# Row parts of the PE array taken in turn on two PSUM banks

## The chip, the core and the metric

The program runs on one core of a Trainium2 chip. The core has five engines that run side by side and wait for each other by semaphores: TensorE (PE, matmuls), VectorE (DVE), ScalarE (ACT), GpSimd (POOL) and SyncE (SP, which starts DMA transfers). Matmuls write to PSUM, which the kernel uses as eight banks of 128 x 512 float32; DVE and ACT read the results from there. The metric is the device time of one execution in microseconds (us), the median of three runs.

## What is computed

Two stacked networks over a sequence of 512 tokens of width 1024, all in float32. The first block has two layers: a dilated band attention beside an attention over 256 memory rows, then a gated delta rule beside the same memory attention, each followed by a gated feed-forward. The second block mixes a gated linear attention, a state space scan and a sparse attention. Four places matter here:

```
# delta stage, for each of 6 heads, 8 chunks of 64 tokens and 2 directions
a = lmat + eye(64)                       # lmat strictly lower triangular
sol = triangular_solve(a, rhs, lower=True, unit_diagonal=True)

# dilated band attention, 12 heads of 64 in 3 groups
logits = einsum('nbqhd,nbkhd->nbhqk', qs, kw)

# memory attention, 4 heads of 64 over 256 rows, in both layers
logits = einsum('bshd,bmhd->bhsm', q, k)

# gated linear attention, 4 heads of 32
scores = einsum('bhnid,bhnjd,bhnijd->bhnij', qh, kh, decay)
```

## The kernel before

Weights stream from memory through three raw buffers (SP issues the transfers), are split into a high and a low part (ACT L239, DVE L258) and multiplied by the activations in three matmuls for each product (L267 to L269, PSUM tiles named `bk`). These projections, feed-forwards and output products are most of PE's work. Between them stand the small stages.

**What sets the order.** Nothing is scheduled by the tools: a planner in the kernel (`Flow`) runs generators. Each `yield "PE", cost` (or DVE, ACT, POOL) asks for an engine with an estimated cost in us, `yield "get", "lv"` asks for a PSUM bank of a set, `F.put` gives it back. The planner takes the request that can start first and, among those within 0.1 us, the one with the smallest `late`. The order it finds is the program's order on each engine. The eight banks are divided into sets: mm 2 (projections), px 3, lv 3. All small stages here take their banks from lv.

**The array's parts.** A matmul with 64 contracted rows uses half the rows of PE's array (partitions 0 to 63 or 64 to 127: a row part); one with 64 output columns uses half its columns. Heads of 64 lie on one row part each, heads of 32 on a quarter of the rows.

**The inverse (`inverse`, L1480).** The unit triangular systems of a head are inverted by doubling: U holds the inverses' diagonal blocks, and each of five levels computes products of Ln and U (L1528, 16 matmuls of 64x64x64: eight on row part f=0 into one bank, then eight on f=1 into another), transposes U (L1509, four 128x128, a third bank `tt`), copies both (ACT: `xs` twice 256 columns L1536, `T` 512 columns L1516), multiplies the transposes by the products (L1547, again eight matmuls on one row part into one bank, then eight on the other into another) and writes the result into U under a mask (DVE, L1552, once for each bank). A last half level (L1565, L1571, L1585) makes the off-diagonal half for `Uf`. There is one U at a time (`inv=1`), so the six heads follow each other. The chains over chunks (`chain`), the convolutions (`hn`, L1316), the memory attention and the projections of later heads run in between.

**The other three.** The attention's unit (L653) and the memory attention (L851) take for each of two row parts h a bank, two matmuls (columns 128, 192 or 256), and DVE's pass over it. The linear attention's scores (L2121) take for each of four heads on 32 rows a bank and eight matmuls of 32x64x64 (four at level 6).

Of the kernel before, what the change touches and what calls it, by code (L numbers as in the profile page):

```python
# [26 lines left out]
F32 = mybir.dt.float32  # L27
# [28 lines left out]
class Flow:  # L56
# [42 lines left out]
    def run(self):  # L99
        while self.threads:  # L100
            again = True
            while again:
                again = False
                for t in list(self.threads):
                    kind, *arg = t["req"]
                    value = None
                    if kind == "get" and any(self.sets[n] for n in arg):
                        value = min((n for n in arg if self.sets[n]), key=lambda n: min(self.sets[n])[0])
                        tok = min(self.sets[value])
                        self.sets[value].remove(tok)  # L110
                    elif kind == "wait" and all(e["tok"] for e in arg):
# [47 lines left out]
class K:  # L159
# [375 lines left out]
    def attention(self, F, W, eX, eM, eB, at, e2):  # L535
# [98 lines left out]
        def unit(g, t):  # L634
# [202 lines left out]
    def mem_attention(self, F, i, q, tile_p, tile_t, aux, acc):  # L837
        nc = self.nc
        for t in range(4):
# [5 lines left out]
            for h in range(2):  # L845
                rr = slice(h * 64, h * 64 + 64)
                yield "get", aux
                yield "PE", 0.86
                s = self.psum(aux, "ms_s").rearrange("p (c k) -> p c k", c=2)
                for c in range(2):  # L850
                    nc.tensor.matmul(s[:, c, :], q[rr, c, ts], self.memK[i][rr, c, :], start=True, stop=True)  # L851
                yield "DVE", 0.6
# [309 lines left out]
    def deltanet(self, F, wev, order, eX, res):  # L1162
# [313 lines left out]
        QQ = 0.063  # L1476

        def inverse(h, r):
# [23 lines left out]
            def transposes():  # L1502
                yield "get", "lv"
                tt = yield "PE", 4 * TR, tU
                t = self.psum("lv", "tt")
# [5 lines left out]
                return t, tt  # L1511

            def copyT(t, tt):
                tT = yield *act(512), tt
                T = late["pool"].tile([P, 2, 2, 2, 64], F32, name="T")
                nc.scalar.activation(T.rearrange("p d n f q -> p (d n f q)"), t, AF.Copy)  # L1516
                F.put("lv", tT)
                return T, tT
            dn8 = lambda x: x[:, :256].rearrange("p (d n q) -> p d n q", d=2, n=2)
            for l in range(1, 6):  # L1520
                X2, tx, xs = [], [], []
                for f in range(2):
                    yield "get", "lv"
                    tx.append((yield "PE", 8 * QQ, tU))
                    x = self.psum("lv", "x2")
                    for d in range(2):
                        for c in range(4):
                            nc.tensor.matmul(dn8(x)[HB[c % 2], d, c // 2, :], Ln[d][HB[f], c, HB[f]],  # L1528
                                             U[HB[f], d, c, :], start=True, stop=True)
                    X2.append(x)  # L1530
                t, tt = yield from transposes()
                ts = []
                for f in range(2):
                    ts.append((yield *act(256), tx[f]))
                    xs.append(late["pool"].tile([P, 2, 2, 64], F32, name=f"xs{f}"))
                    nc.scalar.activation(xs[f], dn8(X2[f]), AF.Copy)  # L1536
                    F.put("lv", ts[f])
                T, tT = yield from copyT(t, tt)
                ty, ys = [], []
                for par in range(2):  # L1540
                    yield "get", "lv"
                    ty.append((yield "PE", 8 * QQ, *ts, tT))
                    y = self.psum("lv", "y2")
                    for d in range(2):
                        for n in range(2):
                            for f in range(2):
                                nc.tensor.matmul(dn8(y)[HB[f], d, n, :], T[HB[par], d, n, f, :],  # L1547
                                                 xs[f][HB[par], d, n, :], start=True, stop=True)
                    ys.append(y)
                for par in range(2):  # L1550
                    tU = yield "DVE", 0.34, ty[par]
# [5 lines left out]
            xs = late["pool"].tile([P, 2, 2, 64], F32, name="xs0")  # L1557
            X2, tx, ts = [], [], []
            for d in range(2):
                f = 1 - d  # L1560
                yield "get", "lv"
                tx.append((yield "PE", 4 * QQ, tU))
                x = self.psum("lv", "x2")
                for c in range(4):
                    nc.tensor.matmul(dn8(x)[HB[c % 2], 0, c // 2, :], Ln[d][HB[f], c, HB[1 - f]], U[HB[f], d, c, :],  # L1565
                                     start=True, stop=True)
# [1744 lines left out]
```

## Time and profile before

| | us |
|---|---|
| median of 3 runs | 1822.44 (1821.06 to 1831.11) |
| profiled execution | 1820.18 |
| its span, first to last instruction | 1818.5 |
| attention stage, about | 78 to 262 |
| delta stage, first products to the last `Uf` | 720 to 1018 |
| linear attention's scores | 1494 to 1560 |

A row of PE's instructions in order has the start, the time from its start to the end of the last of it, the line, the operation, what is written from what, the used rows*columns of the array, the moving operand and the count; neighbouring instructions of a line are one row. An fp32 matmul is two instructions there. A row of a stretch has busy us and, in brackets, the instructions that touch it. PEld is PE's loading of the stationary operand, which overlaps with PE.

### The profile page before, as it was taken

The numbers are of one execution on the slowest core, as the hardware profiler recorded it, in microseconds if no ns is written. First come the engines' busy times: TensorE is split into PE (matmuls) and PEld (weight loads), VectorE is DVE, ScalarE is ACT, GpSimd is POOL, SyncE is SP. The second block draws the span as 40 slices with busy tenths as digits, with TensorE's granted clock in tenths as the row PEclk, the third lists the DMA queues.
The fourth block names the chain that finished last, engine by engine and source line by source line (L and its number), as shares of the span: only waits on it lengthen the run. The fifth ranks groups of instructions, "written<-read, shape, count | busy, mean of one in ns | idle before, by whom it ended". The sixth has DMA issues, their size and how long they took to land.

```text
span 1818.5 us, 30258 instructions
## 1 busy us (share of the span) xinstructions
PE 1762.9 (97%) x12031; PEld 1465.8 (81%) x12031; DVE 976.7 (54%) x1997; ACT 768.2 (42%) x1844; POOL 337.9 (19%) x496
## 2 busy tenths in 40 slices
PE   6999989999999998999999999999999999999999
PEld 5988779888888887887878778888888888887787
DVE  6333556323333378665776466454433566467673
ACT  6434435332222355555655344333223352344671
POOL 5200001000000021121122252275540032210000
PEclk9999999999999999999999999999999999999999
DMA  6422133333333233101011155344333253552112
GB/s 202 137 58 82 47 115 93 117 93 101 97 93 95 92 116 82 36 25 47 25 36 36 36 145 152 100 145 136 108 106 93 86 154 91 156 139 70 33 36 82
DMA packets 211982, 167.85 MB, mean 92 GB/s; under 512 B 21996, under 2 KB 183036, under 8 KB 211840
## 3 DMA queue, kind: packets, MB, share of 16 engines
q1 hardware_dynamic: 203808, 154.39, 28.9%
q0 software_dynamic: 4560, 9.42, 2.0%
q10 hardware_dynamic: 3472, 2.10, 0.4%
q8 instruction: 95, 1.56, 0.4%
q14 instruction: 47, 0.39, 0.1%
HBM read 152.23 MB, written 13.65 MB: 91 GB/s over the span
## 4 chain that ended last, share of the span: by engine, by line
PE 87%; DVE 7%; ACT 2%; issue 2%; DMA 1%; POOL 1%; ACTq 0%; SPq 0%; DVEq 0%; POOLq 0%
PE bk L267 23%; PE bk L268 22%; PE bk L269 21%; PE x L1528 2%; PE y L1547 2%; PE no L2765 1%; DVE wl L258 1%; DVE hn L1316 1%; PE npT L2748 1%; PE gs L2121 1%; PE tt L1509 1%; PE ms_s L851 1%; DVE hs L934 1%; PE ns L2734 1%; PE ns L2732 1%
## 5 line engine op out<-in xcount | busy, mean ns | idle before, releaser
L258 DVE TENSOR_TENSOR wl<-raw,wh 128x512 fp32r<-128x512 f32 x450 | 315.6, 741 | 372.4 <-ACT wh L239 371.8
L239 ACT ACTIVATE wh<-raw 128x512 fp32r<-128x512 f32 x474 | 272.8, 622 | 549.8 <-PE bk L269 311.1
L267 PE MATMUL bk<-Xh,wl 128*128 128x512 f32 (+2 forms) x1312 | 495.3, 378 | 0.2 <-ACT Xh L943 0.2
L268 PE MATMUL bk<-Xl,wh 128*128 128x512 f32 (+2 forms) x1312 | 478.3, 365 | 0.5 <-DVE Xl L948 0.5
L269 PE MATMUL bk<-Xh,wh 128*128 128x512 f32 (+2 forms) x1312 | 478.5, 365 | 0.0
L267 PEld LDWEIGHTS bk<-Xh,wl 128*128 128x128 f32 (+1 forms) x1312 | 247.2, 188 | 41.6 <-issue 5.1
L269 PEld LDWEIGHTS bk<-Xh,wh 128*128 128x128 f32 (+1 forms) x1312 | 247.0, 188 | 40.1
L268 PEld LDWEIGHTS bk<-Xl,wh 128*128 128x128 f32 (+1 forms) x1312 | 247.5, 189 | 34.8 <-DVE Xl L948 0.9
L267 PE MATMUL bk<-wh,Xl 128*128 128x512 f32 (+1 forms) x424 | 155.5, 367 | 8.5 <-ACT wh L239 3.5
L268 PE MATMUL bk<-wl,Xh 128*128 128x512 f32 (+1 forms) x424 | 146.3, 345 | 0.1
L269 PE MATMUL bk<-wh,Xh 128*128 128x512 f32 (+1 forms) x424 | 146.2, 345 | 0.0
L267 PE MATMUL bk<-wh,Al 128*128 128x512 f32 x352 | 139.7, 397 | 0.0
L268 PE MATMUL bk<-wl,Ah 128*128 128x512 f32 x352 | 139.5, 396 | 0.0
L269 PE MATMUL bk<-wh,Ah 128*128 128x512 f32 x352 | 138.6, 394 | 0.0
L913 POOL TENSOR_TENSOR nc<-ncm,nhalf 128x1 f32<-128x1 f32 x16 | 11.6, 722 | 676.5 <-DVE ncm L911 672.2
L267 PEld LDWEIGHTS bk<-wh,Xl 128*128 128x128 f32 x424 | 85.6, 202 | 21.5 <-issue 4.1
L1085 DVE TENSOR_TENSOR sg<-sg,bk 128x512 f32<-128x512 f32 x44 | 30.2, 687 | 124.2 <-PE bk L269 119.7
L268 PEld LDWEIGHTS bk<-wl,Xh 128*128 128x128 f32 x424 | 85.8, 202 | 7.7 <-DVE wl L258 0.9
L269 PEld LDWEIGHTS bk<-wh,Xh 128*128 128x128 f32 x424 | 85.4, 201 | 8.0
L267 PEld LDWEIGHTS bk<-wh,Al 128*128 128x128 f32 x352 | 66.1, 188 | 16.1
L269 PEld LDWEIGHTS bk<-wh,Ah 128*128 128x128 f32 x352 | 66.0, 188 | 16.0
L268 PEld LDWEIGHTS bk<-wl,Ah 128*128 128x128 f32 x352 | 66.1, 188 | 15.4
(588 smaller groups left out, 2673.2 us busy)
## 6 DMA issues: line engine op xcount, KB each, us to landing
raw<-in_ffn_w_gate_up_dram SPq DMA_DIRECT2D x88, 512.0 KB, 4.0
raw<-in_ffn_w_down_dram SPq DMA_DIRECT2D x44, 512.0 KB, 3.4
raw<-in_dn_w_in_dram SPq DMA_DIRECT2D x27, 512.0 KB, 3.8
raw<-in_att_w_in_dram SPq DMA_DIRECT2D x20, 512.0 KB, 3.8
raw<-in_w_in_dram SPq DMA_DIRECT2D x20, 512.0 KB, 4.2
raw<-in_mem_w_kv_dram SPq DMA_DIRECT2D x8, 512.0 KB, 3.6
raw<-in_att_w_out_dram SPq DMA_DIRECT2D x8, 512.0 KB, 3.5
xd<-x SPq DMA_DIRECT2D x8, 512.0 KB, 3.0
```

The lines of the kernel that those rows point to most:

```text
L239: nc.scalar.activation(wh[:, sl], ev["raw"][:, sl], AF.Copy)
L258: eng.tensor_tensor(wl[:, sl], raw[:, sl], wh[:, sl].bitcast(F32), op=OP.subtract)
L267: mm(out, A[1], B[0], start=first, stop=False, **kw)
L268: mm(out, A[0], B[1], start=False, stop=False, **kw)
L269: mm(out, A[0], B[0], start=False, stop=last, **kw)
L851: nc.tensor.matmul(s[:, c, :], q[rr, c, ts], self.memK[i][rr, c, :], start=True, stop=True)
L934: nc.vector.scalar_tensor_tensor(hh[:, hv[i]], x[:, t, hv[i]], r2, r["gain"][:, hv[i]], op0=OP.mult, op1=OP.mult)
L1085: nc.vector.tensor_tensor(sg, sg, pu, op=OP.mult)
L1316: nc.vector.scalar_tensor_tensor(acc[:, d0:d1], raw[:, d0 + o:d1 + o], cw[:, ti, tap:tap + 1], acc[:, d0:d1], op0=OP.mult, op1=OP.add)
L1509: nc.tensor.transpose(t[:, i:i + P], U[:, d, 2 * n:2 * n + 2, :].rearrange("p c q -> p (c q)"), self.ident)
L1528: nc.tensor.matmul(dn8(x)[HB[c % 2], d, c // 2, :], Ln[d][HB[f], c, HB[f]], U[HB[f], d, c, :], start=True, stop=True)
L1547: nc.tensor.matmul(dn8(y)[HB[f], d, n, :], T[HB[par], d, n, f, :], xs[f][HB[par], d, n, :], start=True, stop=True)
```

## The change

The planner gets a new request, `"two"`, which is granted when a set has two free banks and takes both. At the four places the matmuls of both row parts become one piece of work: they are written in turn, first row part into one bank, second row part into the other.

- Inverse: the 16 first products alternate between the row parts and banks. The transposes of U go into the upper 256 columns of the same two banks (L1523 in the changed file) in place of a third one. ACT then copies each bank whole, products and transposes, into `xT0` and `xT1` (L1530; 384 columns in the last level). The second products (L1544) alternate too.
- Attention, memory attention: both h in one piece, c outside, h inside.
- Linear attention: heads two by two, the pair innermost.
- The planner's costs of these pieces are set lower. In `chain` the addition into `ot` names the other direction's copy as something it waits for.

```diff
+                    elif kind == "two" and len(self.sets[arg[0]]) > 1:
+                        for _ in range(2):
+                            tok = min(self.sets[arg[0]])
+                            self.sets[arg[0]].remove(tok)
...
-            for h in range(2):
-                yield "get", "lv"
-                yield "PE", 2 * 0.0017 * (hi - lo)
-                s = self.psum("lv", "as").rearrange("p (c k) -> p c k", c=2)
-                rr = slice(h * 64, h * 64 + 64)
-                for c in range(2):
-                    nc.tensor.matmul(s[:, c, lo:hi], qT[rr, c, ts], kT[rr, c, k0 + lo:k0 + hi], start=True, stop=True)
-                tk = yield dve(2 * (hi - lo))
+            yield "two", "lv"
+            tp = yield "PE", 2 * 0.0018 * (hi - lo)
+            sh = [self.psum("lv", "as").rearrange("p (c k) -> p c k", c=2) for _ in range(2)]
+            for c in range(2):
+                for h in range(2):
+                    rr = slice(h * 64, h * 64 + 64)
+                    nc.tensor.matmul(sh[h][:, c, lo:hi], qT[rr, c, ts], kT[rr, c, k0 + lo:k0 + hi], start=True, stop=True)
+            for h, s in enumerate(sh):
+                tk = yield *dve(2 * (hi - lo)), tp
...
-        QQ = 0.063
+        QQ = 0.035
...
+            def step(products):
+                yield "two", "lv"
+                tt = yield "PE", len(products) * QQ + 4 * TR, tU
+                b = [self.psum("lv", "x2") for _ in range(2)]
+                for i, at, lhsT, rhs in products:
+                    nc.tensor.matmul(dn8(b[i])[at], lhsT, rhs, start=True, stop=True)
                 for d in range(2):
                     for n in range(2):
-                        i = (2 * d + n) * P
-                        nc.tensor.transpose(t[:, i:i + P], U[:, d, 2 * n:2 * n + 2, :].rearrange("p c q -> p (c q)"),
+                        o = 256 + n * P
+                        nc.tensor.transpose(b[d][:, o:o + P], U[:, d, 2 * n:2 * n + 2, :].rearrange("p c q -> p (c q)"),
                                             self.ident)
...
+                lo = 512 - 256 - 16 * len(products)
+                for i in range(2):
+                    ts.append((yield *act(512 - lo), tt))
+                    z.append(late["pool"].tile([P, S], F32, name=f"xT{i}"))
+                    nc.scalar.activation(z[i][:, lo:], b[i][:, lo:], AF.Copy)
+                    F.put("lv", ts[i])
...
+                xs, T, ts = yield from step([(f, (HB[c % 2], d, c // 2), Ln[d][HB[f], c, HB[f]], U[HB[f], d, c, :])
+                                             for d in range(2) for c in range(4) for f in range(2)])
+                yield "two", "lv"
+                ty = yield "PE", 16 * QQ, *ts
+                ys = [self.psum("lv", "y2") for _ in range(2)]
+                for d in range(2):
+                    for n in range(2):
+                        for f in range(2):
+                            for par in range(2):
+                                nc.tensor.matmul(dn8(ys[par])[HB[f], d, n, :], T[d][HB[par], n, f, :],
+                                                 xs[f][HB[par], d, n, :], start=True, stop=True)
...
-                    yield "get", "lv"
-                    tp = yield "PE", 0.25
-                    p = self.psum("lv", "gs").rearrange("p (u k) -> p u k", k=64)[:, :4]
+                    if not h % 2:
+                        yield "two", "lv"
+                        tp = yield "PE", 0.3 if l == 6 else 0.5
+                        pp = [self.psum("lv", "gs").rearrange("p (u k) -> p u k", k=64)[:, :4] for _ in range(2)]
```

How the order moves, at three places. PE at the first head's first level, before (`x` the first products, the number is the bank's; `tt` the transposes; `y` the second products):

```order
L1528 MATMUL x_5849<-U,Ln_5692 64x64 x4
L1528 MATMUL x_5849<-U,Ln_5814 64x64 x4
L1528 MATMUL x_5861<-U,Ln_5692 64x64 x4
L1528 MATMUL x_5861<-U,Ln_5814 64x64 x4
L1509 MATMUL tt<-ident,U 128x128 x4
L1327 MATMUL pkT<-ident,ktok 128x128 x4
L275 MATMUL rowbc<-ident,gc 128x128 x4
L1547 MATMUL y_5898<-xs_5876,T 64x64
L1547 MATMUL y_5898<-xs_5878,T 64x64
```

and now, from the end of the same products on:

```order
L1519 MATMUL x_5849<-U,Ln_5814 64x64
L1519 MATMUL x_5850<-U,Ln_5814 64x64
L1523 MATMUL x_5849<-ident,U 128x128 x2
L1523 MATMUL x_5850<-ident,U 128x128 x2
L1335 MATMUL pkT<-ident,ktok 128x128 x4
L279 MATMUL rowbc<-ident,gc 128x128 x4
L271 MATMUL bk<-Xh,wl 128x512
L272 MATMUL bk<-Xl,wh 128x512
L273 MATMUL bk<-Xh,wh 128x512
L1544 MATMUL y_5898<-xT_5880 64x64
L1544 MATMUL y_5899<-xT_5880 64x64
```

The products go to two banks (5849 and 5850) by turns instead of eight and eight, the transposes to the same two; a projection stands ahead of the second products where none stood. ACT at the same place, before:

```order
L1311 ACTIVATE hn<-craw,convw 128x512
L1536 ACTIVATE xs_5876<-x_5849 128x256
L1536 ACTIVATE xs_5878<-x_5861 128x256
L1516 ACTIVATE T<-tt 128x512
L1367 ACTIVATE kTh<-pkT 128x512
L1307 ACTIVATE craw<-bk 128x512
```

and now:

```order
L1319 ACTIVATE hn<-craw,convw 128x512
L1530 ACTIVATE xT_5880<-x_5849 128x512
L1530 ACTIVATE xT_5889<-x_5850 128x512
L1375 ACTIVATE kTh<-pkT 128x512
L1315 ACTIVATE craw<-bk 128x512
```

Two copies of 512 columns stand for two of 256 and one of 512. PE at the last head's fifth level, just ahead of its second products, before (`poT` is another head's output; three more projection matmuls stand between the transposes and these rows):

```order
L267 MATMUL bk<-Xh,wl 128x512
L268 MATMUL bk<-Xl,wh 128x512
L269 MATMUL bk<-Xh,wh 128x512
L1327 MATMUL poT<-ident,otok 128x128 x4
L1547 MATMUL y_9641<-xs_9623,T 64x64
```

and now:

```order
L1519 MATMUL x_9527<-U,Ln_9087 64x64
L1519 MATMUL x_9528<-U,Ln_9087 64x64
L1523 MATMUL x_9527<-ident,U 128x128 x2
L1523 MATMUL x_9528<-ident,U 128x128 x2
L1544 MATMUL y_9561<-xT_9553 64x64
```

Ahead of the second products six projection matmuls and a transpose stood; now nothing stands there.

## Rows read from the trace of the kernel before

**Rows 1.** The page: busy time of each engine; the chain that ended last.

```profile
PE 1762.9 (97%) x12031; PEld 1465.8 (81%) x12031; DVE 976.7 (54%) x1997; ACT 768.2 (42%) x1844; POOL 337.9 (19%) x496
PE 87%; DVE 7%; ACT 2%; issue 2%; DMA 1%; POOL 1%; ACTq 0%; SPq 0%; DVEq 0%; POOLq 0%
```

**Rows 2.** Stretches: start:end and length, then busy us (instructions) PE, PEld, DVE, ACT, POOL; clock; DMA.

```profile
720.00:1018.00 298.00, 289.55 (x3436) 236.06 (x3435) 204.81 (x475) 162.97 (x462) 64.81 (x54) 1.00 0.12 35
1494.00:1560.00 66.00, 66.00 (x778) 54.19 (x777) 41.94 (x97) 20.92 (x43) 20.18 (x22) 1.00 0.36 102
```

**Rows 3.** PE's instructions in order: start us, busy us; the last level's products.

```profile
749.60 0.47 PE L1565 MATMUL x<-U,Ln 64*64 64x64 f32 x16
751.98 0.45 PE L1585 MATMUL y<-xs,T 64*64 64x64 f32 x8
```

**Rows 4.** PE's instructions in order, the attention's scores.

```profile
92.14 1.13 PE L653 MATMUL as<-kT,qT 64*128 64x256 f32 x4
94.53 1.13 PE L653 MATMUL as<-kT,qT 64*128 64x256 f32 x8
97.94 0.91 PE L653 MATMUL as<-kT,qT 64*128 64x192 f32 x4
...
144.81 1.16 PE L653 MATMUL as<-kT,qT 64*128 64x128 f32 x8
...
153.83 0.71 PE L653 MATMUL as<-kT,qT 64*128 64x128 f32 x4
```

**Rows 5.** PE's instructions in order, the inverse's first products: a whole pair, a half.

```profile
733.77 0.98 PE L1528 MATMUL x<-U,Ln 64*64 64x64 f32 x32
...
770.08 0.68 PE L1528 MATMUL x<-U,Ln 64*64 64x64 f32 x16
```

**Rows 6.** PE's busy us (instructions) in the delta stage: L1528, then L1547, then L1585.

```profile
720.00:1018.00 298.00, 33.28 (x960) 1.00 0.12 35
720.00:1018.00 298.00, 32.37 (x960) 1.00 0.12 35
720.00:1018.00 298.00, 4.96 (x96) 1.00 0.12 35
```

**Rows 7.** PE, PEld busy us (instructions): two rows of L653, then three of L851.

```profile
78.00:262.00 184.00, 16.03 (x96) 11.72 (x96) 0.98 0.21 64
208.00:262.00 54.00, 4.81 (x32) 3.66 (x32) 0.94 0.13 41
...
78.00:262.00 184.00, 8.92 (x32) 5.35 (x32) 0.98 0.21 64
208.00:262.00 54.00, 3.28 (x12) 2.01 (x12) 0.94 0.13 41
720.00:1018.00 298.00, 9.02 (x32) 5.35 (x32) 1.00 0.12 35
```

**Rows 8.** PE: a memory score, a linear attention's score; all of L2121, as rows 7.

```profile
831.50 1.13 PE L851 MATMUL ms_s<-memK,oT 64*128 64x256 f32 x4
...
1494.60 0.68 PE L2121 MATMUL gs<-gq,gk 32*64 32x64 f32 x16
...
1494.00:1560.00 66.00, 21.75 (x480) 17.32 (x480) 1.00 0.36 102
```

**Rows 9.** Groups on xs, T and U: duration ns min/median/max, first and last start, forms.

```profile
L1536 ACT ACTIVATE xs<-x x60: 357/383/421, 722.3 to 1009.6; 128x256 f32<-128x256 f32 x60
...
L1516 ACT ACTIVATE T<-tt x36: 585/597/618, 723.1 to 1014.8; 128x512 f32<-128x512 f32 x36
...
L1552 DVE COPY_PREDICATED U<-lm,y x60: 430/443/455, 727.2 to 1013.0; 128x256 f32<-128x256 uint8 x60
```

**Rows 10.** A stretch at the attention stage's end, columns as in rows 2.

```profile
208.00:235.00 27.00, 21.66 (x191) 16.84 (x190) 20.90 (x55) 15.39 (x59) 0.00 (x0) 0.94 0.07 21
```

**Rows 11.** A piece of the chain (start, us); a wait (us, times, longest); delta stage.

```profile
794.55 1.68 DVE hn L1316
...
PEld x L1528 <- DVE U L1552: 4.1, 7, 1.9
```

More of the change, by code (lines that the diff above doesn't have):

```diff
@@ L844, in mem_attention @@
             den = self.small.tile([P, 4], F32, name="mden")
[L845 to L852, printed above, removed]
+            yield "two", aux
+            tp = yield "PE", 0.95
+            sh = [self.psum(aux, "ms_s").rearrange("p (c k) -> p c k", c=2) for _ in range(2)]
+            for c in range(2):
+                for h in range(2):
+                    rr = slice(h * 64, h * 64 + 64)
+                    nc.tensor.matmul(sh[h][:, c, :], q[rr, c, ts], self.memK[i][rr, c, :], start=True, stop=True)
+            for h, s in enumerate(sh):
+                yield "DVE", 0.6, tp
                 nc.vector.tensor_reduce(nm[:, h::2], s, axis=AX.X, op=OP.max, negate=True)
@@ L1506, in transposes @@
                 for d in range(2):
                     for n in range(2):
-                        i = (2 * d + n) * P
-                        nc.tensor.transpose(t[:, i:i + P], U[:, d, 2 * n:2 * n + 2, :].rearrange("p c q -> p (c q)"),
+                        o = 256 + n * P
+                        nc.tensor.transpose(b[d][:, o:o + P], U[:, d, 2 * n:2 * n + 2, :].rearrange("p c q -> p (c q)"),
                                             self.ident)
[L1511 to L1518, printed above, removed]
+                z, ts = [], []
@@ L1520, in inverse @@
             for l in range(1, 6):
[L1521 to L1539, printed above, removed]
-                for par in range(2):
[L1541 to L1549, printed above, removed]
@@ L1552, in inverse @@
+                for par in range(2):
+                    tU = yield "DVE", 0.34, ty
                     nc.vector.copy_predicated(U[:, :, par::2, :],
@@ L1556, in inverse @@
             b4 = beta.rearrange("p (d c h) -> p d c h", d=2, c=4)[:, :, :, h]
[L1557 to L1566, printed above, removed]
-                X2.append(x)
-            t, tt = yield from transposes()
-            for d in range(2):
-                ts.append((yield *act(128), tx[d]))
-                nc.scalar.activation(xs[:, d], dn8(X2[d])[:, 0], AF.Copy)
-                F.put("lv", ts[d])
-            T, tT = yield from copyT(t, tt)
+            xs, T, ts = yield from step([(d, (HB[c % 2], 1, c // 2), Ln[d][HB[1 - d], c, HB[d]], U[HB[1 - d], d, c, :])
+                                         for c in range(4) for d in range(2)])
             yield "get", "uf"
@@ L1595, in inverse @@
             r["eU"]["tok"] = max(t, tP)
-            r["n"], r["done"] = 0, set()
+            r["n"], r["done"] = 0, {}
             r["o"] = late["pool"].tile([P, 4, P], F32, name="otok", bufs=2)
@@ L1644, in chain @@
                 if c in r["done"]:
-                    to = yield "DVE", 0.2, to
+                    tc_ = yield "wait", r["done"][c]
+                    to = yield "DVE", 0.2, to, tc_
                     nc.vector.tensor_tensor(ot[:, c, :], ot[:, c, :], o, op=OP.add)
                 else:
-                    r["done"].add(c)
+                    done = r["done"][c] = F.event()
                     to = yield *act(P), to
                     nc.scalar.activation(ot[:, c, :], o, AF.Copy)
+                    done["tok"] = to
                 F.put("lv", to)
```

40 lines of the change are left out of this document (19 added, 21 removed).

## The prediction, made before the run

> **What bounds the kernel now.** I read the page first: TensorE (PE) is busy 97% of the span, and 87% of the chain that ended last goes through it [rows 1]. VectorE (DVE) is busy 54%, ScalarE (ACT) 42%, so the question in each touched stage is whether PE is held up there by its own work. The stretches say yes: over the 298 us of the delta stage PE is busy 289.6, over the 66 us of the linear attention's scores 66.0 [rows 2]. The one exception is the end of the attention stage, where PE is busy only 21.7 of 27 us and DVE 20.9 [rows 10]. The granted clock is 1.00 in the first two stretches, so no clock is to be won or lost there.
>
> Next: what does a small matmul cost PE? In the inverse a matmul uses 64 of the 128 rows and 64 of the 128 columns of the array, and an fp32 matmul is two instructions in the trace. The half step at L1585 (8 instructions, one row part, one bank) occupies PE for 0.45 us. L1565 is 16 instructions, 8 on one row part and 8 on the other, into two banks, and occupies PE for 0.47 us [rows 3]. Twice the work for 0.02 more: **the row parts run side by side when both are within reach.** The attention's scores show the same without any change of code: where two groups of four on *different* row parts happen to stand next to each other (94.53 us; the heads' loop tells the parts) the eight take 1.13 us, as long as the four at 92.14 alone; where two groups on the *same* row part stand together (144.81 us) eight take 1.16 against 0.71 for four of that width, which is one after the other [rows 4]. And a whole pair of the inverse (32 instructions) takes 0.98, while a pair cut by other work takes 0.68 twice [rows 5]: with all of one bank's matmuls first, PE gets to the second row part only when most of the first is done. With perfect overlap a pair should take 0.68 + 0.03 = 0.71 us, where 0.03 is the 0.02 above, rounded up.
>
> **What the new order takes away.** I price every pair at the busy time of one half plus 0.03 us.
>
> - First products (L1528): 33.28 us now for 960 instructions [rows 6]; 30 pairs (6 heads, 5 levels) at 0.71 are 21.3. Gain 12.0.
> - Second products (L1547): 32.37 now, as many pairs, 21.3 afterwards. Gain 11.1.
> - Last level: L1585 4.96 now; six pairs of 0.48 are 2.9. Gain 2.1. L1565 (six times 0.47) is side by side already: no gain.
> - Memory scores: 8.92 + 9.02 us [rows 7]; a half is 1.13 [rows 8], eight pairs of 1.16 are 9.3. Gain 8.6, about half of it in each stage.
> - Attention scores: 16.03 us [rows 7]. Two of its twelve pairs are 192 wide (0.91), two 256 wide (1.13), eight 128 wide (0.71) [rows 4]: 2 x 0.94 + 2 x 1.16 + 8 x 0.74 = 10.1. Gain 5.9.
> - Linear attention's scores: 21.75 us for 32 groups of 0.68 [rows 8]; 16 pairs of 0.71 are 11.4. Gain 10.4. No row here shows two parts of 32 rows side by side, so its ends are 10.4 (as the parts of 64 rows) and 0; I take the first, since its halves run at exactly the pace of the 64-row ones (16 instructions in 0.68 in both).
>
> The sum is 50.1 us of PE's time: 25 from the inverse, 4.4 more in the delta stage from the memory, 10.2 in the attention stage, 10.4 at the scores.
>
> **What it adds and moves.** The transposes of U now go into the second half of the two product banks: the same four instructions behind the products, no cost. The copies: before, two of 0.383 us and one of 0.597 on ACT; now two of 128x512, 0.597 each as the copy to T [rows 9]. That is 0.17 us less ACT work per step, but both now begin behind the transposes, and the second products wait for both. From the last transpose to the second products that makes about 0.2 + 0.6 + 0.6 = 1.4 us (0.2 is the planner's own figure for a hop between engines); from those to the next first products two updates of U at 0.443 [rows 9] and two hops, about 1.3. Whether PE waits depends on what the planner put between. In the changed program's order I counted the other PE work in these gaps, a bk matmul 128x512 at 0.23 and a 128x128 one at 0.11: nearly all hold 1.1 to 3.5 us, as much as is needed, and the total of other work from the first to the last step is as before. Only the last head runs short: one gap of 0 and two near 0.7, because the projections that fill PE are used up ahead of its last two steps. That costs about 3 us. PE waits for the inverse little today (4.1 us for U's update, [rows 11]); I allow 1 us more.
>
> Not everything in the delta stage follows PE. Between heads the chain leaves it for the convolution on DVE (single pieces of 1.7 us, [rows 11]); with less PE work these stretches come to the front oftener: 3 us. In the tail of the attention stage, where DVE and PE take turns, as scores worth 1.9 us and memory scores worth 1.5 fall [rows 10]: 4.81 and 3.28 us there [rows 7], less four pairs of 0.74 and one and a half of 1.16; I count half, so 1.7 are lost. Against 50.1 stand 3 + 1 + 3 + 1.7, and 1.3 for waits inside the first pairs, which the 33.28 contains and which stay: 10 us. **Net 40 us: 1820.2 - 40 = 1780.** The median of the runs shown is 2.3 us above the profiled execution, which is less than the uncertainty of this sum; I leave the number as it is.
>
> The wait in "done" (second direction's addition behind the first one's copy) only tells the planner of an order that the data had already. Nothing is added on the chip.
>
> One thing has to hold for all of this: a matmul on the second row part must be able to start ahead of one that stands before it in the program. In L1565 the program has all eight instructions of the first bank ahead of the second bank's, and 0.47 us for both [rows 3] is possible only so. The Trainium skill says otherwise: by "TensorE: Matmul & The Clock Gate", Part 3, What overlaps and what doesn't, matmuls start and end strictly in program order. By it the result would be the second rival's. The rows disagree with it, and the measurement decides.
>
> **The rivals.**
> 1. *The inverse's own chain becomes the bound of the delta stage.* It is serial (one U, three lv banks); a step has about 0.7 + 0.5 + 1.4 + 0.7 + 1.3 = 4.6 us in it, and the 36 steps make 166 of the 298 us, the rest being PE's other work and the change of heads. For it: DVE pieces on the chain [rows 11], the exhausted fill at the last head. Against: PE busy 97% there and the filled gaps. If two thirds of the delta stage's 29 us stay behind, the time is 1820 - (50 - 19 - 2) = 1791, with bad luck 1800.
> 2. *Alternating parts don't run side by side*, each start waiting for its predecessor's. Then the two instructions of a matmul, 0.058 us apart ((0.68 - 0.45) / 4, from the halves of 16 and 8 instructions on two column parts, [rows 3, 5]), hold up the next part, and a pair takes 0.68 + 8 x 0.058 = 1.14 us. An uncut pair now takes 0.98, a cut one 1.36; in the order of before 43 of the 60 are uncut, which makes 43 x 0.16 - 17 x 0.22 = +3 us, and the scores give back about as much: 1820, no change. The measured pieces speak against it [rows 3, 4].
> 3. *Slower: two banks at once of three lv banks.* A pair starts only when two are free, and the memory attention and the chains' outputs hold single ones (a memory score bank through 1.13 of PE, a maximum and two exponentials). 72 pairs of the inverse stand behind this; it decides from 50 / 72 = 0.7 us of unfilled wait at each, and at 1 us each the time is 1820 - 50 + 72 = 1842. For it: at the third head, where the memory runs, gaps grow to 5 and 6 us in the new order. Against: these are full of other PE work, not empty. The Trainium skill's "TensorEngine Tiling (Array Packing)", Gotcha 1, names this pressure on PSUM; no row here shows its price.
> 4. *All of it arrives*, the off-PE stretches shrinking with PE's, and the order falling well elsewhere: 1820 - 50 = 1770, at best 1765.
>
> **How the numbers follow.** Forecast (1773 to 1787) 0.53; rival 1 (1788 to 1805) 0.24; rival 4 (1764 to 1772) 0.13; rival 2 (1812 to 1824) 0.06; rival 3 0.04. The likeliest's time is 1780. The range takes in rivals 1 and 4 and thereby the zero end of the 32-row parts alone (1790): 1765 to 1803. A measurement of this kernel tells about 0.5% from no change, 9 us: below 1813 lie the first three cases, 0.90; same 0.06; slower 0.04.
>
> **What would show it.** Products of a pair: 32 instructions in about 0.71 us with none of 0.98 or twice 0.68, scores of the linear attention 32 in 0.71, memory scores eight in 1.16. If the pairs are short but the delta stage (298 us) does not shrink to about 276, PE's idle time there or longer waits of the products for ACT or DVE name rival 1. Pairs of 1.1 us name rival 2. Idle PE ahead of the first of a pair, ended by the release of a bank, names rival 3. The forecast is wrong if the stages before and after the touched ones move by more than 5 us, since I gave the reshuffled order there nothing.

## The result and the profile after

The changed kernel takes **1762.9 us** (median of 4 runs, 1761.48 to 1763.83) against 1822.9 (4 runs, 1821.06 to 1831.11): ratio 0.966, interval 0.963 to 0.969. The forecast was 1780 with a range down to 1765: the direction and the mechanism in the touched pieces were right, the gain is 20 us larger, and the time lies 2 us outside the range. (A run with a lower mean granted clock is longer, for the kernel before 1820.78 us at 0.992 and 1831.65 at 0.984; the ratios leave disturbed runs out, which are six of the ten of "before, measured costs" below, 1843.8 to 1848.0 us at 0.969 to 0.972, and medians in us of different experiments compare only to a few us.)

The profiled execution took 1761.48 us, its span 1759.5 against 1818.5. The page of the changed kernel, busy time and the chain that ended last, answers to [rows 1]:

```profile
PE 1708.7 (97%) x12031; PEld 1423.2 (81%) x12031; DVE 979.8 (56%) x1997; ACT 763.2 (43%) x1808; POOL 338.0 (19%) x496
PE 84%; DVE 9%; ACT 2%; issue 2%; DMA 1%; POOL 1%; ACTq 0%; SPq 0%; DVEq 0%; POOLq 0%
```

PE's busy time fell by 54.2 us, and its idle time (span less busy) from 55.6 to 50.8. Together that is the 59.0 us of the span. DVE's share of the chain rose from 7 to 9%: a little of the path went over to it, no more.

Where the time went, by stretches: first the kernel before, from the start to the first product, the delta stage, up to the linear attention's scores, the scores, the rest (columns as in [rows 2]).

```profile
0.00:720.00 720.00, 690.68 (x3712) 578.53 (x3712) 335.61 (x598) 283.45 (x644) 60.70 (x85) 0.99 0.34 101
720.00:1016.00 296.00, 289.09 (x3434) 235.76 (x3433) 202.85 (x471) 161.20 (x459) 64.81 (x54) 1.00 0.13 35
1016.00:1494.00 478.00, 466.61 (x2287) 389.94 (x2288) 247.57 (x505) 176.36 (x355) 174.91 (x318) 0.99 0.40 117
1494.00:1560.00 66.00, 66.00 (x778) 54.19 (x777) 41.94 (x97) 20.92 (x43) 20.18 (x22) 1.00 0.36 102
1560.00:1818.50 258.50, 250.54 (x1825) 207.37 (x1824) 148.76 (x329) 126.28 (x349) 17.29 (x18) 0.99 0.30 83
```

The same five stretches of the changed kernel:

```profile
0.00:708.00 708.00, 680.19 (x3712) 570.27 (x3712) 333.48 (x598) 284.51 (x643) 60.59 (x84) 0.99 0.35 103
708.00:982.00 274.00, 263.58 (x3444) 215.35 (x3442) 209.86 (x475) 157.24 (x427) 65.85 (x54) 0.99 0.14 40
982.00:1451.00 469.00, 462.20 (x2292) 386.42 (x2282) 244.99 (x501) 174.89 (x350) 173.75 (x318) 1.00 0.41 119
1451.00:1501.00 50.00, 49.36 (x741) 42.38 (x739) 40.54 (x90) 18.49 (x38) 19.73 (x21) 1.00 0.36 106
1501.00:1759.50 258.50, 253.38 (x1857) 208.74 (x1856) 150.92 (x336) 128.06 (x353) 18.05 (x19) 1.00 0.31 88
```

The stretches are shorter by 12, 22, 9, 16 and 0 us. The delta stage gave the 22 us of the forecast. Its idle time grew by 3.5 (6.9 to 10.4) as it is cut here, which in the kernel before is 2.4 us ahead of the last `Uf`; from the first product to the last `Uf` in both kernels it grew by 1.6 (8.8 to 10.4). The first stretch gave 12 where 8.5 were forecast, and the third, in which nothing was changed, gave 9: 4.4 of busy time and 4.6 of idle time. The fourth holds 37 instructions fewer and the fifth 32 more, work that went over, so those two are read together: 16 us against a forecast of 10.4.

For the third stretch two experiments from below help, in which the kernel before keeps all its work and only the planner's costs differ. From the last `Uf` to the first score, the kernel before and the one with measured costs:

```profile
1018.40:1494.60 476.20, 466.75 (x2289) 390.11 (x2289) 245.85 (x500) 175.16 (x351) 174.91 (x318) 0.99 0.41 118
1022.20:1490.70 468.50, 461.14 (x2281) 385.55 (x2280) 243.38 (x496) 174.41 (x349) 173.74 (x318) 1.00 0.41 119
```

With 0.069 a product it is 469.9 us, in the changed kernel 467.7. So most of these 9 us can be had by another order, without row parts. The stage ahead of it, from the first product to the last `Uf`, took 298.3, 295.2 and 303.4 us in the three kernels without row parts, both together 774.5, 763.7 and 773.3: how much of the 9 us is a true gain of the change is open.

From the first score to the end, the kernel before and the one with the linear attention's scores alone changed:

```profile
1494.60:1818.50 323.90, 315.94 (x2596) 261.09 (x2595) 190.09 (x425) 146.62 (x390) 37.48 (x40) 0.99 0.31 87
1495.50:1803.90 308.40, 302.64 (x2596) 251.12 (x2595) 191.60 (x425) 146.62 (x390) 37.81 (x40) 1.00 0.32 91
```

The changed kernel has the same 308.40 and 302.64 us there. So this part gives 15.5 us by itself, 13.3 of busy and 2.2 of idle time, where its score instructions give 10.7 (below).

The pieces themselves, PE's instructions of the changed kernel in order (as [rows 3 to 5, 8]): a whole pair of first products, an attention's and a memory attention's scores, the linear attention's scores.

```profile
721.07 0.69 PE L1519 MATMUL x<-U,Ln 64*64 64x64 f32 x32
...
95.93 1.13 PE L658 MATMUL as<-kT,qT 64*128 64x256 f32 x8
...
796.31 1.13 PE L858 MATMUL ms_s<-memK,oT 64*128 64x256 f32 x8
...
1451.08 0.69 PE L2108 MATMUL gs<-gq,gk 32*64 32x64 f32 x32
```

Every pair takes as long as one half did alone: 0.69 for 32 instructions where 16 took 0.68, 1.13 for eight where four took 1.13. PE's busy time by line follows (L1519, which holds the last level's 96 too, then L1544, L1566; L858 in both stages; L658; L2108), to be read against [rows 6 to 8]:

```profile
708.00:982.00 274.00, 24.52 (x1056) 19.32 (x1056) 0.99 0.14 40
708.00:982.00 274.00, 21.15 (x960) 16.91 (x960) 0.99 0.14 40
708.00:982.00 274.00, 2.71 (x96) 2.02 (x96) 0.99 0.14 40
78.00:262.00 184.00, 4.54 (x32) 2.75 (x32) 0.99 0.27 83
708.00:982.00 274.00, 4.54 (x32) 2.75 (x32) 0.99 0.14 40
78.00:262.00 184.00, 10.10 (x96) 6.90 (x96) 0.99 0.27 83
1450.00:1502.00 52.00, 11.07 (x480) 8.86 (x480) 1.00 0.37 114
```

| | forecast gain | measured |
|---|---|---|
| first products (33.28 and six times 0.47 before) | 12.0 | 11.6 |
| second products | 11.1 | 11.2 |
| last level | 2.1 | 2.3 |
| memory scores, both layers | 8.6 | 8.9 |
| attention scores | 5.9 | 5.9 |
| linear attention's scores | 10.4 | 10.7 |
| sum | 50.1 | 50.6 |

So the gross gain is right to 0.5 us, and the 20 us lie elsewhere: the forecast took 10 off for waits, while PE's idle time in fact fell by 4.8 us and PE was busy for 3.6 us less with work that was not touched.

### The profile page after: what moved, and what is told of

It reads as the page before. It is cut to its first block, busy times and chain, and to the rows that moved or that the text cites. A ratio compares the mean times of both kernels' runs of the same rounds, so it can differ in the third digit from the quotient of the medians.

```text
span 1759.5 us, 30190 instructions
## 1 busy us (share of the span) xinstructions
PE 1708.7 (97%) x12031; PEld 1423.2 (81%) x12031; DVE 979.8 (56%) x1997; ACT 763.2 (43%) x1808; POOL 338.0 (19%) x496
## 4 chain that ended last, share of the span: by engine, by line
PE 84%; DVE 9%; ACT 2%; issue 2%; DMA 1%; POOL 1%; ACTq 0%; SPq 0%; DVEq 0%; POOLq 0%
PE bk L271 23%; PE bk L272 22%; PE bk L273 22%; DVE hn L1324 2%; DVE wl L262 1%; PE no L2753 1%; PE npT L2736 1%; PE x L1519 1%; PE x L1523 1%; PE y L1544 1%; DVE hs L942 1%; PE ns L2722 1%; PE hT L949 1%; PE ns L2720 1%; PE o L1625 1%
```

## The experiments

Twelve kernels. The table has the profiled execution of each: span, PE's busy time (both from the page), their difference, and the mean granted clock; beside it the median of the runs and the ratio to the kernel before on the same chip.

| kernel | runs, us | ratio (interval) | span | PE busy | PE idle | clock |
|---|---|---|---|---|---|---|
| before | 1822.9 | 1 | 1818.5 | 1762.9 | 55.6 | 0.992 |
| after | 1762.9 | 0.966 (0.963 to 0.969) | 1759.5 | 1708.7 | 50.8 | 0.993 |
| inverse alone | 1796.1 | 0.985 (0.981 to 0.989) | 1798.1 | 1742.4 | 55.7 | 0.988 |
| linear attention's scores alone | 1806.3 | 0.991 (0.989 to 0.993) | 1803.9 | 1749.4 | 54.5 | 0.992 |
| attention alone | 1818.5 | 0.997 (0.996 to 0.998) | 1818.4 | 1761.5 | 56.9 | 0.989 |
| memory alone | 1816.9 | 0.996 (0.995 to 0.998) | 1815.4 | 1758.2 | 57.2 | 0.991 |
| attention and memory | 1808.1 | 0.990 (0.986 to 0.993) | 1805.3 | 1749.5 | 55.8 | 0.991 |
| after, in blocks | 1783.0 | 0.977 (0.974 to 0.980) | 1778.4 | 1728.6 | 49.8 | 0.993 |
| after, copies twice | 1793.8 | 0.983 (0.980 to 0.986) | 1793.2 | 1724.0 | 69.2 | 0.984 |
| after, cut once more | 1770.8 | 0.970 (0.967 to 0.973) | 1769.9 | 1720.4 | 49.5 | 0.990 |
| after, measured costs | 1787.8 | 0.980 (0.976 to 0.983) | 1785.8 | 1720.0 | 65.8 | 0.985 |
| after, 0.031 a product | 1771.5 | 0.970 (0.966 to 0.974) | 1770.1 | 1712.0 | 58.1 | 0.989 |
| before, measured costs | 1826.6 (four runs, 1813.9 to 1839.4; profiled 1813.9) | 1.000 (0.996 to 1.005) | 1812.0 | 1763.0 | 49.0 | 0.989 |
| before, 0.069 a product | 1824.8 | 0.998 (0.995 to 1.000) | 1824.5 | 1771.7 | 52.8 | 0.986 |

### Does the order inside a pair make the gain?

Everything of the change stays, the two banks, the larger copies, the planner's order; only the loops are turned, so that one row part's matmuls all stand ahead of the other's. Two of the seven places:

```diff
-            for c in range(2):
-                for h in range(2):
+            for h in range(2):
+                for c in range(2):
...
-                                             for d in range(2) for c in range(4) for f in range(2)])
+                                             for f in range(2) for d in range(2) for c in range(4)])
```

> The changed kernel with the same pieces in the same order on every engine, but inside a piece of PE's all matmuls of one row part first, then all of the other. Theory A (PE reaches a second row part only some six instructions ahead, so long blocks lose the overlap): a pair of the inverse or of the linear attention's scores goes from 0.70 back to 0.98 us, 60 x 0.28 + 14 x 0.28 = 21 us; the short blocks of the attention, the memory and the last level (8 instructions or fewer) lose nothing: 1784. Rival: what the change wins comes from larger pieces (fewer changes of shape, a better order), not from the turns: the time stays within 5 us of 1763.

It took 1783.0 us. A pair of first products, and the busy time of the first, second and linear attention's products, in this kernel:

```profile
721.53 0.98 PE L1519 MATMUL x<-U,Ln 64*64 64x64 f32 x32
...
708.00:998.00 290.00, 32.66 (x1056) 27.44 (x1056) 0.98 0.13 38
708.00:998.00 290.00, 29.60 (x960) 25.33 (x960) 0.98 0.13 38
1466.00:1521.00 55.00, 15.57 (x480) 13.36 (x480) 1.00 0.35 106
```

0.98 us is the price of an uncut pair before [rows 5], and the three lines hold 21.1 us more than the changed kernel's, the span 18.9. With the same instructions in the same banks, taking the parts in turn is worth these 20 us. The expectation's 1784 is met; the short blocks lose little (attention 10.39 against 10.10, memory 4.56 against 4.54 in each layer). The other 40 come with the rest of the change, that is with joining both parts into one piece, so that nothing stands between them, with the lower costs and with the order that follows; these were not separated here. This also shows the limit of what overtakes what: a second part that stands eight matmuls further on starts late, the next one at once. By the starts of the single instructions the second part of the pair at 721.53 begins 0.29 us behind the first, when ten of the first part's 16 instructions have started. The kernel before shows the overtaking itself: in its pair at 733.77 [rows 5] the instruction that signals the first bank is the 16th in the program and the 21st to start.

### Each part alone

The planner's new request and one part of the change, the rest as before (hunks as shown above; QQ 0.035 and the addition's new wait in `chain` go with the inverse).

> The kernel before with the delta stage's inverse alone changed. Theory A (what a part wins is PE time: its pairs run side by side, and every piece of small matmuls saved also spares its successor about 0.10 us): first and second products 22.7 us less, 22 pieces fewer, together 25 us: 1798. Theory B (the surplus of the whole change over the prediction is a lucky order, or the parts need each other): the inverse alone gives the predicted 25 less its 7 of waits, 18 us: 1805.

> The kernel before with the linear attention's scores alone changed. Theory A: 9.6 us on the scores and 16 pieces fewer at 0.10: 11 us, 1812. Theory B: 10.4 us as predicted or less, with a spread of some us by the order.

> The kernel before with the attention's scores alone changed. Theory A: 5.2 us and 5 pieces at 0.10: 5.7 us, 1817. Theory B: the tail of the attention stage, where PE waits for DVE, takes a third of that back: 4 us, 1819.

> The kernel before with the memory attention's scores alone changed, in both layers. Theory A: 8.0 us and 9 pieces at 0.10: 9 us, 1814. Theory B: half of the attention stage's 4 us is lost in its tail: 7 us, 1816. If the four parts add up to the whole (60 us), they don't need each other.

Measured by medians: 27, 17, 4.6 and 6.2 us less, 55 of the 60 in all. The inverse lies by its first account (1798), the memory by its second (1816); the attention's two accounts are too close together for its 1818.5 to decide. The scores alone are 6 us faster than either account had (1812): their stretch to the end gives 15.5 us, as shown with the result. The inverse alone took 1790 to 1806 us, so one run of four gained less (17.5 us) than its profile's 20.5 us of busy time, and its profile shows why the difference is not to be read too finely. Stretches of that kernel at the linear attention's scores:

```profile
1484.00:1490.00 6.00, 6.00 (x82) 5.46 (x81) 3.83 (x12) 0.38 (x1) 1.24 (x2) 1.00 0.01 3
1490.00:1496.00 6.00, 6.00 (x55) 5.30 (x56) 1.27 (x4) 0.65 (x2) 1.65 (x3) 0.61 0.36 112
1496.00:1502.00 6.00, 6.00 (x41) 4.53 (x42) 3.32 (x7) 3.07 (x6) 0.42 (x1) 0.50 0.00 0
1502.00:1508.00 6.00, 6.00 (x45) 5.19 (x43) 2.01 (x7) 0.39 (x1) 1.73 (x4) 0.75 0.35 93
```

PE is busy throughout, yet the granted clock (last column but two) falls from 2.4 to 1.2 GHz for most of these 18 us: 6 x 0.39 + 6 x 0.50 + 6 x 0.25 = 6.8 us are lost there, by an estimate that takes the same work as half as long at full clock. What ran ahead were the small score products and projections of the unchanged kind. The kernel before and the changed one have a clock of 1.00 in this stage in their profiles.

### The attention stage's end

Attention and memory alone moved the first product of the delta stage forward by 1.3 and 3.3 us, the whole change by 12. So both together, without the rest:

> The kernel before with the attention's and the memory attention's scores changed together. Alone they gave 4.6 and 6.2 us, and moved the first product of the delta stage forward by 1.3 and 3.3 us, while in the changed kernel it comes 11.9 earlier. Theory A (they help each other at the attention stage's end, where DVE and PE take turns): first product of the delta stage at about 708 us, time about 1807. Theory B (the gains add): first product at 715.5, time about 1812.

1808.1 us, and the first product at 708.0. PE's last wait of the attention stage, for DVE's `Xl` (start, us, the idle time before it in brackets), in the kernel before:

```profile
246.09 0.80 PE L267 MATMUL bk<-wh,Xl 128*128 128x512 f32 x1 [2.61 <-DVE Xl L790]
```

with the attention's scores alone:

```profile
244.58 0.79 PE L271 MATMUL bk<-wh,Xl 128*128 128x512 f32 x1 [2.72 <-DVE Xl L796]
```

with the memory attention's scores alone:

```profile
243.88 0.50 PE L271 MATMUL bk<-wh,Xl 128*128 128x512 f32 x1 [1.67 <-DVE Xl L794]
```

and with both:

```profile
234.81 0.50 PE L271 MATMUL bk<-wh,Xl 128*128 128x512 f32 x1 [2.81 <-DVE Xl L796]
```

One alone gains 1.5 or 2.2 us there, both gain 11.3. Their PE time (14.8 us in both layers) adds; the tail's waits do not: PE is idle for 6.9, 9.7, 8.2 and 5.5 us of the stretch from 208 to 245 in these four. (The reading is rough: the stretch holds more of the work behind the tail where the tail ends earlier, and with the attention's scores alone the lower clock takes about 3 us more ahead of the first product than in the kernel before, 10.3 against 7.3 by the estimate explained below.) The forecast had written off half of what falls in the tail; in the changed kernel nothing of it is lost. Whether the order that the planner found there or the shorter scores make the tail short was not separated.

### Is the delta stage bound by the inverse's own chain?

In the changed kernel each of the two copies of a step is made twice, one after the other, and the planner is told:

```diff
+                    ts[i] = yield *act(512 - lo), ts[i]
+                    nc.scalar.activation(z[i][:, lo:], b[i][:, lo:], AF.Copy)
```

> The changed kernel with each of ACT's copies xT made twice (the planner knows of it): 72 more copies of 0.6 us, 1.2 us more in each of the 36 steps of the serial inverse. If PE's work bounds the delta stage, the planner fills the longer gaps and little is lost: 1763 to 1775. If the inverse's own chain bounds it, as the first rival of the prediction had it, 36 x 1.2 = 43 us come on top: 1800 or more.

1793.8 us, 31 more. What PE waited for in the delta stage (us in total, times, longest), first in the changed kernel:

```profile
PE chain L1612 <- DVE vs L1610: 5.3, 5, 1.4
PE y L1544 <- ACT xT L1530: 1.1, 2, 0.9
...
PE x L1519 <- DVE U L1548: 0.4, 1, 0.4
```

and with the copies doubled:

```profile
PE y L1546 <- ACT xT L1532: 5.9, 5, 2.1
PE x L1519 <- DVE U L1550: 4.4, 9, 0.8
```

The first rival is thus not what happened (the waits for the inverse are 1.1 and 0.4 us), but it stands close by: 36 steps lengthened by two copies of 0.6 us, 43 us of chain, come out as 31, between the two cases of the expectation. Of the 33.7 us of span 18.4 are PE's idle time and about 12 the lower clock (23.1 against 11.3, by the estimate explained below), so other work still filled a part of the 43. The fill between the steps is enough, as the count in the forecast said, with little to spare.

### What does an order cost?

The planner's costs are estimates, and no duration on the chip hangs on them, only the order. First the costs set to what the pieces took, in the changed kernel, then in the one before (there 0.057 for QQ, and the same three others); then QQ alone, by 0.004 and 0.006 the other way.

```diff
-            tp = yield "PE", 2 * 0.0018 * (hi - lo)
+            tp = yield "PE", 0.22 + 0.0033 * (hi - lo)
-            tp = yield "PE", 0.95
+            tp = yield "PE", 1.06
-        QQ = 0.035
+        QQ = 0.039
-                        tp = yield "PE", 0.3 if l == 6 else 0.5
+                        tp = yield "PE", 0.61
```

> The changed kernel with the planner's costs of the changed pieces set to the measured ones (QQ 0.039, attention 0.22 + 0.0033 a column, memory 1.06, scores 0.61): another order, the same work. If the surplus over the prediction is a lucky order, this falls back by some 5 to 15 us, 1768 to 1778; if it is the work itself, it stays within 4 us: 1759 to 1767.

> The kernel before with the planner's costs of the same pieces set to the measured ones (QQ 0.057, attention 0.22 + 0.0033 a column, memory 1.06, scores 0.61). The same question from the other side: if the kernel before has an unlucky order, another one is faster by 5 to 15 us, 1808 to 1818; if not, it stays within 5 us of 1823.

> The changed kernel with another planner's cost for one product of the inverse, 0.031 in place of 0.035 us: the same instructions in another order. Theory A (an order costs what it leaves PE idle, and what the granted clock loses behind such a wait): between 1760 and 1795, and against the changed kernel's profile the difference of the spans is that of PE's idle time plus that of the work at the lower clock, within 3 us. Theory B (an order costs by its changes of shape): the time differs while idle time and clock don't.

> The kernel before with another planner's cost for one product of the inverse, 0.069 in place of 0.063 us: the same instructions in another order. It gives the spread of the kernel before by its order alone. Theory A (the gain of the change stands well above that spread): 1812 to 1835. Theory B (the 60 us are in part a bad order of before): below 1805.

Better estimates made the changed kernel 25 us slower; 0.031 in place of 0.035 made it 9 us slower (7 by the ratios). The first is 10 us more than the expectation's upper end for a lucky order. Of the 26.3 us of span of the first, 15.0 are PE's idle time. Most of the other 11.3 goes by the clock, as one place shows. PE's instructions in order there:

```profile
1508.35 1.12 PE L2346 MATMUL s5y<-q,wB 128*128 128x64 f32 x4 [3.93 <-DVE q L2327]
1509.40 1.13 PE L2108 MATMUL gs<-ge 32*64 32x64 f32 x32
```

and the stretches behind it:

```profile
1508.00:1512.00 4.00, 3.65 (x43) 3.42 (x44) 3.60 (x10) 1.21 (x2) 0.45 (x1) 0.50 0.49 137
1512.00:1516.00 4.00, 4.00 (x45) 3.66 (x46) 2.19 (x5) 0.59 (x1) 3.84 (x3) 0.50 0.33 98
1516.00:1520.00 4.00, 4.00 (x47) 3.66 (x46) 0.99 (x3) 1.33 (x7) 0.36 (x1) 0.50 0.51 135
1520.00:1524.00 4.00, 4.00 (x23) 2.92 (x24) 1.46 (x5) 0.41 (x1) 0.35 (x1) 0.57 0.00 0
```

PE waits 3.93 us for DVE, and then the granted clock is 0.50, the level of 1.2 GHz, for some 15 us: the same 32 score instructions take 1.13 us in place of 0.69. If the same busy time were half as long at full clock, this wait of 3.9 us is followed by 3.65 x 0.5 + 4 x 0.5 + 4 x 0.5 + 4 x 0.43 = 7.5 us more. Summed over the whole span (busy time in stretches of 3 us times what the clock lacks of 1), the lower clock by this estimate costs the kernel before 13.3 us, the changed one 11.3, the one with measured costs 22.0, the one with 0.031 14.6. With that, 15.0 + 10.7 of 26.3 us and 7.3 + 3.3 of 10.6 would be accounted for: an order costs the idle time that it leaves, and, by the estimate, the clock behind it. The estimate is rough by some us: up to the first product the kernel cut once more (below) runs PE's instructions in the order of the changed one, the estimate gives it 3.7 us more there, and its first product comes 1.1 us later. The kernel before has a smaller spread of idle time (49.0 to 55.6 us in three orders), and its ratios moved by 0.2% at most, with intervals of up to half a per cent. With measured costs its runs lie far apart, though, and the profiled one is 6.5 us of span below the kernel before, by 6.6 us less idle time. Whether the order of the kernel before is an unlucky one, as the expectation asked, is therefore not settled; its third stretch, shown with the result, says that it is in part.

### Does a change of shape cost something?

In the traces the first interval of a piece that follows another kind of piece is longer: behind the pair at 721.07 the transposes and the projections go on as follows.

```profile
721.70 0.66 PE L1523 MATMUL x<-ident,U 128*128 128x128 f32 x4
722.11 0.48 PE L271 MATMUL bk<-Xh,wl 128*128 128x512 f32 x1
722.42 0.40 PE L272 MATMUL bk<-Xl,wh 128*128 128x512 f32 x1
722.65 0.39 PE L273 MATMUL bk<-Xh,wh 128*128 128x512 f32 x1
```

From start to start the first projection takes 0.31 us, the second 0.23. So in the changed kernel a step's first half was cut once more, same work, same banks, same order around it:

```diff
-                for i, at, lhsT, rhs in products:
-                    nc.tensor.matmul(dn8(b[i])[at], lhsT, rhs, start=True, stop=True)
+                half = len(products) // 2
                 for d in range(2):
+                    for i, at, lhsT, rhs in products[d * half:d * half + half]:
+                        nc.tensor.matmul(dn8(b[i])[at], lhsT, rhs, start=True, stop=True)
                     for n in range(2):
```

> The changed kernel with each step of the inverse cut once more: half of the first products, two transposes, the other half, the other two transposes. The same instructions, the same banks, the same order around them. Theory A (PE pays about 0.10 us each time it goes from small products to a matmul of another shape, as the first interval of the next piece shows in the traces, and the 8.8 us less on untouched work come from fewer such changes): one more change in each of 36 steps, 36 x 0.10 = 3.6 us at the least, twice that if the way back costs as much: 1766 to 1771, with the first transposes behind the products at about 0.21 us to the next start in place of 0.11, now twice in a step. Theory B (no such price; the untouched work got shorter by another order and by the clock): 1763.

1770.8 us, 8 more (6 by the ratios), and the step that took 722.11 - 721.07 = 1.04 us now takes 1.34 (722.43 to 723.77):

```profile
722.43 0.46 PE L1521 MATMUL x<-U,Ln 64*64 64x64 f32 x16
722.82 0.44 PE L1524 MATMUL x<-ident,U 128*128 128x128 f32 x2
723.19 0.46 PE L1521 MATMUL x<-U,Ln 64*64 64x64 f32 x16
723.58 0.44 PE L1524 MATMUL x<-ident,U 128*128 128x128 f32 x2
723.77 0.48 PE L271 MATMUL bk<-Xh,wl 128*128 128x512 f32 x1
```

Two more changes of shape, there and back, cost 0.30 us, 0.15 each, with nothing waiting (PE's idle time is 49.5 against 50.8). In 36 steps that is 10.8 us, and from the first product to the last `Uf` PE's busy time grew by 10.9 (264.8 to 275.7). The whole change does the opposite: it joins pieces, so that in the traces the changed lines' pieces that are followed by another line's fell from 153 to 108. By 0.10 to 0.15 us each (estimated from the two readings above) that is 4.5 to 7 us which the forecast did not have.

## Why the forecast was right and wrong, point by point

- **Row parts side by side.** Right, in all four places, and so is the price of a pair (half plus 0.03; measured half plus 0.01). The rule of the Trainium skill that it was weighed against ("TensorE: Matmul & The Clock Gate", Part 3, What overlaps and what doesn't: starts and ends strictly in program order) would have given the second rival's 1820; the 32 instructions in 0.69 us, the 16th instruction that starts as the 21st and the 20 us between the two loop orders disagree with it.
- **The zero end for parts of 32 rows.** Not needed: 0.69 for 32.
- **Larger, later copies.** Right: the second products waited 1.1 us for `xT` in the whole stage. Doubling them shows that little reserve is left.
- **Waits in the delta stage (3 + 1 + 3 us).** The stage shrank by the forecast 22 us, its idle time grew by 1.6 to 3.5, according to where it is cut, instead of 7. That the length came out is in part luck: the pieces gave 29.6 us there, PE's busy time fell by 25.5, since other work came in and the granted clock, 1.00 before and taken as 1.00 in the forecast, was 0.99 (about 3 us, by the estimate above). Of the 1.3 us for waits inside the first pairs 0.4 stayed (a gain of 11.6 for 12.0). The chains' wait for DVE (`vs`) went from 2.9 to 5.3 us, as expected in kind, not for the convolution that was named; the last head waited 1.1 us for its copies, not 3.
- **The attention's tail (1.7 us lost).** Wrong in sign: nothing lost, 1.8 us gained on top of the 10.2. The experiment with both scores shows the two parts' gains there do not add one by one.
- **Nothing for the reshuffled order elsewhere.** This is the step that failed, and with it that idle time could only grow: 10 us were taken off for waits, and PE's idle time fell by 4.8. From the delta stage to the scores 9 us went, 4.6 of it idle time, most of which the kernel before also gains from other planner costs alone (476.2 to 468.5 and 469.9 us). The stretch behind the scores lost 2.8 us of idle time (8.0 to 5.1), and from the first score to the end 15.5 us went where 10.4 were forecast, with the scores alone as with the whole change. The three orders of the changed kernel that were run leave PE idle for 50.8, 58.1 and 65.8 us and take 1763, 1772 and 1788; the forecast's 55.6 + 8.7 would be near the worst of them. The planner's costs as given happen to make the best order of the three, which is luck. A range of 25 us stood behind a term that I had set to zero, and it goes by idle time and, by the estimate, the clock behind it. Which changes of the order gave the 9 us and the 5 was not tried.
- **Changes of shape.** Not in the forecast; 4.5 to 7 us by the estimate above. Counted from start to start of PE's instructions, where the end of a piece that lies under the next one is not counted twice, the pieces gave 46.1 us and the untouched work 8.1 (a count that differs a little from the 8.8 of the expectation). Of the 8.1 the clock has 2.0 by the estimate (13.3 to 11.3), and the rest is of the size of the estimate; the kernel cut once more shows the price, the sum was not tried by itself.
- **Rivals.** The first was not met but is near; the second and the third are out (no wait of a pair for a bank shows among PE's waits in the delta stage; the kernel in blocks takes two banks at once as well and is 40 us faster than before). The fourth, all of it arrives (1770), was the nearest, and still 7 us short: I had treated 50 us as the upper end, because I allowed the idle time only to grow.

## What to carry to other kernels

Where a small matmul fills only part of the array, write the parts in turn and as one piece: then PE takes as long as for one part (here fp32, parts of 64 and of 32 rows), and it is saved a change of shape for each piece less. Price such an edit by the piece (that was right to 1%), but give the order that a planner makes of it a range of its own, read from two or three other orders: here 25 us against a gain of 60. And count a wait of PE of several us not by its length alone; look at the granted clock behind it.

## What the runs showed of the hardware that was not expected

In these shapes the time of a group of small matmuls goes by what falls on one part, over rows and columns alike. In the kernel before, the linear attention's level 6 has eight instructions on one row and column part (PE's instructions in order):

```profile
1502.58 0.67 PE L2121 MATMUL gs<-ge 32*64 32x64 f32 x8
```

0.67 for these eight, 0.68 for the sixteen on two column parts of the other levels [rows 8], and 0.69 for the 32 on four parts of the changed kernel.

The overtaking has a short reach: with eight matmuls of the first part ahead a pair takes 0.98 us, with the parts in turn 0.69, and the second part starts only when ten of the first's 16 instructions have started. A change from small products to a matmul of another shape and back costs 0.30 us. And the granted clock fell to its lower level for some 15 us both behind a wait of 3.93 us and, in the kernel with the inverse alone, with PE busy throughout.
